# Shift and scale from transposed weights, and layer 0's input projection in skewed blocks

## The chip, the cores and the metric

The kernel runs on one core of one Trainium2 chip. The metric is the device time of one execution in microseconds (us). A core has a matrix engine (TensorE, PE in the profile; its weight loads are PEld), a vector engine (VectorE, DVE), an activation engine (ScalarE, ACT), GpSimd (POOL) and SyncE (SP), which here issues nearly all transfers from one queue, in order. Matrix products are accumulated in PSUM, eight banks of 128 x 512 float32; everything else lies in SBUF, 128 partitions wide.

## The reference

Two layers of an encoder on 256 positions of 2048 channels, all in float32. What the change touches is the modulation: six vectors of 2048 numbers per layer, made from one conditioning vector `c`, of which two pairs (shift and scale) act on a normalised input and two (gates) on a branch's output.

```python
c_act = silu(c)
for l in range(2):
    mod = (c_act @ w_mod[l] + b_mod[l]).reshape(bn, 6, 2048)
    shift_m, scale_m, gate_m, shift_f, scale_f, gate_f = ...
    h = layer_norm(x) * (1 + scale_m) + shift_m
    proj = h @ w_in[l]                    # 4288 columns: U, V, B, E, C, D below
    y = concat(gmlp(U, V), attention(B), short_conv(E, C), conformer_conv(D)) @ w_out[l]
    x = layer_norm(ALPHA * x + (1 + gate_m) * y, post_mix_g[l], post_mix_b[l])
    h = layer_norm(x) * (1 + scale_f) + shift_f
    y = (silu(conv3(h @ w_gate)) * (h @ w_val)) @ w_down[l]
    x = layer_norm(ALPHA * x + (1 + gate_f) * y, post_ffn_g[l], post_ffn_b[l])
```

`w_mod[l]` is 2048 x 12288 float32 (100.7 MB a layer), read once for a single row vector `c_act`.

## The kernel before

**Products.** Contraction runs over KT = 16 blocks of 128 channels (kt 0 to 15). Most weights are loaded into `wraw` tiles and split in two parts, `whi` by a cast on ACT (L437) and `wlo` by a subtraction on DVE (L438); activations are split likewise (`hT`, L457, L458), and each product is three products of the parts. Some weights (`wexact`, L421) are used unsplit in float32. All products are issued by `mm` (L94). Splits go through four `whi` and four `wlo` tiles, which the `wexact` tiles share.

**Raw tiles.** `raw_tile` (L81) hands out four SBUF tiles of 1 MiB in rotation. Weights to be split, modulation weights (`wmod`) and the gain rows of the norms (`gb`) all go through them, and SP issues a load when the tile it takes has been released.

**Modulation.** `mod_step` (L220) adds one block of a vector: weights 128 x width (partition = input channel) times the column `c_act[kt]`, added to a running tile `macc` or `qacc`, one DVE instruction. After 16 steps the partial sums of 128 partitions must be added and turned into columns: `mod_cols` (L170) does it with one matrix product per 128 channels (`ps_mod`), `mod_rows` (L194) with a split, products `ps_row` against ones, a copy `mrow` and four transposes (`ps_mod`, L205). Gates go through `gate_rows` (L265). `mod_stream` (L302) is a generator of steps; `stream` (L380) calls `pump` at each weight load, which takes steps at the phase's rate from `RATES` (L35). What is not ready when a norm wants it is fetched by `need` (L360).

**Layer 0's input projection** (`by_pieces`, L1224) must wait for layer 0's own shift and scale. It works in the five pieces of channels in `PIECES` (L45: 2, 2, 4, 4 and 4 blocks). For each, `mod_piece` (L228) loads 1 MiB units of `w_mod_first`, all 2048 input channels by the piece's columns; half of the first piece's steps are products on PE (`mod_row`, L247). When all units of a piece are in, `sums` turns them, `finish` (L1486) applies them to `hF` (the normalised, transposed input) and splits it, and the piece's products follow: group D (1024 columns) into four held PSUM banks, groups U, V, E (512 each) and, in the first four blocks, B (768) into banks that are copied out (`side`, L1252). D is unsplit for kt 0 to 3, U, V, E for kt 0 to 11. Groups B and C (L1344, L1351) follow with the mixers' own work, and then `out_proj`.

**Hand-over.** `out_proj` (L645) ends a layer half with a norm on DVE; `first_group` (L595) turns the result (`to_hT`, L566, transposes `ps_xT`, L576) and starts the next products. L571 to L573 make the first activation of each turn wait for the modulation. In layer 0's FFN the last four blocks (kt from LATE_KT = 12) of shift and scale come later, and `late` (L1390) does these blocks' products afterwards.

The instructions are put in order on each engine by the framework's scheduler, mostly near the order of the program; an engine runs its own in order.

Of the kernel before, what the change touches and what calls it, by code (L numbers as in the profile page):

```python
# [13 lines left out]
P = 128  # L14
D = 2048
# [20 lines left out]
    dict(B=1.634, C=1.9, out=1.7, first=1.2, up=0.68, down=0.83),  # L36
# [7 lines left out]

PIECES = ((0, 2), (2, 2), (4, 4), (8, 4), (12, 4))  # L45
# [9 lines left out]
LEAD = (2, 3, 1, 2, 2)  # L55
# [10 lines left out]
def encoder_kernel(ctx: ExitStack, tc: tile.TileContext, A: dict, consts: bass.AP, out: bass.AP):  # L66
# [83 lines left out]

    PM = []
# [16 lines left out]
    MOD, MOD_BY = {}, {}  # L168

    def mod_cols(l, m, k0, acc, row=None):  # L170

        n = acc.shape[1] // P
        ps = ms_tile("ps_mod")
        mm(ps[:, 0:n], ident, bcol[l][:, m * KT + k0 : m * KT + k0 + n], True, False)
        for j in range(n):
            mm(ps[:, j : j + 1], acc[:, j * P : (j + 1) * P], ones[:, 0:1], False, row is None)
            if row is not None:
                mm(ps[:, j : j + 1], row[:, j * P : (j + 1) * P], ones[0:1, 0:1], False, True)
        cols = keep.tile([P, n], F32, name=f"mod_{l}_{m}_{k0}")
        if m in (SHIFT_M, SHIFT_F):  # L180
            done = act.copy(cols, ps[:, 0:n])
        else:
            done = ident_act(cols, ps[:, 0:n], 1.0, ones[:, 0:1])
        for j in range(n):
            MOD[(l, m, k0 + j)] = cols[:, j : j + 1]
            MOD_BY[(l, m, k0 + j)] = done.ins.name
# [6 lines left out]

    def mod_rows(l, m, acc, n=4):  # L194

        ps = ms_tile("ps_row")
        parts = [x for c0 in range(0, n * 512, 1024) for x in halves(acc, c0, min(1024, n * 512 - c0))]
        for j, pair in enumerate(parts):
            for i, part in enumerate(pair):
                mm(ps[0:4, :], onesR[:, P + 4 * j : P + 4 * j + 4], part, j + i == 0, j + i == n)  # L200
        row = tmp_tile("mrow")
        act.copy(row[0:4, :], ps[0:4, :])
        ps = ms_tile("ps_mod")
        for i in range(4):
            pe.transpose(ps[:, 4 * i : 4 * i + 4], row[0:4, i * P : (i + 1) * P], ident[0:4, 0:4])  # L205
        cols = keep.tile([P, KT], F32, name=f"mod_{l}_{m}")
        done = dve.scalar_tensor_tensor(
            out=cols.rearrange("p (i j) -> p i j", i=4)[:, :, :n],
            in0=ps[:, 0:KT].rearrange("p (i j) -> p i j", i=4)[:, :, :n],
            scalar=0.0 if m in (SHIFT_M, SHIFT_F) else 1.0,  # L210
            in1=bcol[l][:, m * KT : m * KT + 4 * n].rearrange("p (j i) -> p i j", i=4),
            op0=ALU.add,
            op1=ALU.add,
        )
        for k in range(4 * n):
            at = 4 * (k % 4) + k // 4
            MOD[(l, m, k)] = cols[:, at : at + 1]
            MOD_BY[(l, m, k)] = done.ins.name
# [8 lines left out]

    def mod_piece(l, ms, k0, nkt, shared=False):  # L228


        n, width = len(ms), nkt * P
        nk = 2048 // (n * width)
        acc = tmpp.tile([P, D], F32, tag="macc", name="qacc", bufs=2)[:, : n * width]
        units = []
        box = {}

        def unit(u):
            raw = raw_tile("wmod").rearrange("p (k m c) -> p k m c", k=nk, m=n)
            nc.sync.dma_start(
                out=raw.rearrange("p k m c -> p (k m c)"), in_=A["w_mod_first"][16 * k0 * n * P // 2048 + u]  # L240
            )
            for k in range(nk):
                kt, w = u * nk + k, raw[:, k, :, :].rearrange("p m c -> p (m c)")
                if shared and k >= nk // 2:
                    if u == 0 and k == nk // 2:
                        box["row"] = acc_tile("mod_row")
                    mm(box["row"][0:1, :], cact[:, kt : kt + 1], w, u == 0 and k == nk // 2, kt == KT - 1)  # L247
                else:
                    mod_step(acc, w, kt, kt == 0)

        for u in range(KT // nk):
            units.append(lambda u=u: unit(u))

        def sums():
            row = None
            if shared:
                row = tmp_tile("mod_row")
                act.copy(row[0:1, :], box["row"][0:1, :])
            for i, m in enumerate(ms):
                at = slice(i * width, (i + 1) * width)  # L260
                mod_cols(l, m, k0, acc[:, at], None if row is None else row[0:1, at])

        return units, sums
# [15 lines left out]
    WITH_NORM = {(0, SHIFT_F), (0, SCALE_F), (1, SHIFT_M), (1, SCALE_M)}  # L279

    def settle(i=0):
        l, m, acc, k0, k1 = late.pop(i)
        if m in (GATE_M, GATE_F):
            gate_rows(l, m, acc)
        elif k0 == 0:
            mod_rows(l, m, acc, k1 // 4)
        else:
            mod_cols(l, m, k0, acc[:, k0 * P : k1 * P])

    def late_part(u, v, k0, nk, dst):  # L290
        nc.sync.dma_start(
            out=dst, in_=A["w_mod_late"][v - SHIFT_F, u, :, k0 : k0 + nk, :].rearrange("p k c -> p (k c)")
        )
        return [dst[:, k * 512 : (k + 1) * 512] for k in range(nk)]
# [3 lines left out]
    def load_late_first():  # L298
        for v in (SHIFT_F, SCALE_F):
            late_first[v] = late_part(0, v, 0, 2, slot("wlate")) + late_part(0, v, 2, 2, slot("wlate"))  # L300

    def mod_stream(order):  # L302

        held_back = {}
        for l, m in order:
            if (l, m) == (0, GATE_F):

                for u in range(4):  # L310
                    for v, acc in held_back.items():
                        ws = late_first[v] if u == 0 else late_part(u, v, 0, 4, raw_tile("wmod"))
                        for k in range(4):
                            mod_step(acc[:, LATE_KT * P :], ws[k], 4 * u + k, u + k == 0)
                        if u == 3:
                            late.append((0, v, acc, LATE_KT, KT))
                        yield
            while len(late) >= 2:
                if late[0][:2] in WITH_NORM:
                    yield  # L320
                else:
                    settle()
            acc = tmpp.tile([P, D], F32, tag="macc", name="macc", bufs=2)
            k1 = KT
            if l == 0 and m in (SHIFT_F, SCALE_F):
                held_back[m], k1 = acc, LATE_KT
            w = k1 * P
            for kt in range(KT):
                raw = raw_tile("wmod")
                nc.sync.dma_start(out=raw[:, :w], in_=A["w_mod"][l, kt * P : (kt + 1) * P, m * D : m * D + w])  # L330
                if kt == KT - 1 and m in (GATE_M, GATE_F):
                    row = raw_tile("brow")
                    nc.sync.dma_start(out=row[0:1, :], in_=A["b_mod"][l : l + 1, m * D : (m + 1) * D])
                mod_step(acc[:, :w], raw[:, :w], kt, kt == 0)
                if kt == KT - 1:
                    if m in (GATE_M, GATE_F):
                        dve.tensor_tensor(out=acc[0:1, :], in0=acc[0:1, :], in1=row[0:1, :], op=ALU.add)
                    late.append((l, m, acc, 0, k1))
                    if (l, m) in WITH_NORM:
                        settle(len(late) - 1)  # L340
                yield
                if kt == 1 and late and late[0][:2] not in WITH_NORM:
                    settle()

    mods = mod_stream(
        [(0, GATE_M), (0, SHIFT_F), (0, SCALE_F), (0, GATE_F), (1, SHIFT_F), (1, SCALE_F)]
        + [(1, SHIFT_M), (1, SCALE_M), (1, GATE_M), (1, GATE_F)]
    )
    pace = {"rate": 0.0, "credit": 0.0}

    def phase(l, name):
        pace["rate"] = RATES[l][name]
# [7 lines left out]
    def need(l, m, k1=KT):  # L360
        while (l, m, k1 - 1) not in MOD and (l, m) not in GATE:
            at = [i for i, x in enumerate(late) if x[:2] == (l, m) and x[4] == k1]
            if at:
                settle(at[0])
            else:
                assert next(mods, "end") != "end"
# [1293 lines left out]
```

## Time and profile before

| | us |
|---|---|
| median of 3 runs (2273.24 to 2274.61) | 2274.22 |
| time of the profiled execution | 2276.85 |
| its span, first to last instruction | 2275.1 |
| first product of group D | 28.14 |
| end of layer 0's input projection in pieces, first product of B after it | 190.07 |
| last product of group C, first of layer 0's output projection | 315.39 |

The mean granted TensorE clock of the execution was 0.992. Times below are counted from the span's start. In the profile's rows, "L94 PE MATMUL d<-whi,a 128\*128 128x512" is an instruction on PE issued by line 94, that writes `d` from `whi` and `a`; a part in brackets at the end is idle time ahead of it and what ended it. A float32 product shows as two instructions, a product of split parts as one. 201 MB of the 605 MB moved are modulation weights, by the issues that the page lists (32 and 128 of 1024 KB, 32 of 768 KB, 6 of 1024 KB and 4 of 512 KB).

### The profile page before, as it was taken

The numbers are of one execution on the slowest core, as the hardware profiler recorded it, in microseconds if no ns is written. First come the engines' busy times: TensorE is split into PE (matmuls) and PEld (weight loads), VectorE is DVE, ScalarE is ACT, GpSimd is POOL, SyncE is SP. The second block draws the span as 40 slices with busy tenths as digits, with TensorE's granted clock in tenths as the row PEclk, the third lists the DMA queues.
The fourth block names the chain that finished last, engine by engine and source line by source line (L and its number), as shares of the span: only waits on it lengthen the run. The fifth ranks groups of instructions, "written<-read, shape, count | busy, mean of one in ns | idle before, by whom it ended". The sixth has DMA issues, their size and how long they took to land.

```text
span 2275.1 us, 31298 instructions
## 1 busy us (share of the span) xinstructions
PE 2228.2 (98%) x12316; PEld 1918.6 (84%) x12316; DVE 1770.7 (78%) x2172; ACT 1108.9 (49%) x1655; POOL 25.8 (1%) x49
## 2 busy tenths in 40 slices
PE   7999999999999999999999999999999999999997
PEld 5789886798888888887789899889888888888886
DVE  6678988888888888989977899887675565565676
ACT  3346742354455444544554434545544454454553
POOL 0000000000000000000000000000000000000000
PEclk9999999999999999999999999999999999999999
DMA  9889789678888888898867566774675555555553
GB/s 394 346 358 349 279 318 360 250 288 314 305 308 313 314 321 326 307 335 329 290 237 258 197 232 254 280 262 175 233 258 185 188 188 199 185 188 201 185 186 148
DMA packets 94524, 605.19 MB, mean 266 GB/s; under 512 B 10692, under 2 KB 10884, under 8 KB 31524
## 3 DMA queue, kind: packets, MB, share of 16 engines
q1 hardware_dynamic: 94040, 602.29, 71.9%
q8 instruction: 96, 1.57, 0.3%
q0 software_dynamic: 336, 0.89, 0.1%
q14 instruction: 52, 0.43, 0.1%
HBM read 601.05 MB, written 2.10 MB: 265 GB/s over the span
## 4 chain that ended last, share of the span: by engine, by line
PE 89%; DVE 6%; issue 2%; ACT 2%; DMA 1%; POOL 0%; SPq 0%; DVEq 0%; ACTq 0%; POOLq 0%
PE g_c L94 22%; PE v_c L94 22%; PE d L94 19%; PE o L94 8%; PE D_c L94 4%; PE C_c L94 3%; PE U_c L94 1%; DVE wlo L438 1%; PE U L94 1%; PE V L94 1%; PE B_c L94 1%; DMA wmod<-in_w_mod_dram 1%; PE E_c L94 1%; PE E L94 1%; DVE macc L225 1%
## 5 line engine op out<-in xcount | busy, mean ns | idle before, releaser
L437 ACT CAST whi<-wraw 128x1024 fp32r<-128x1024 f32 (+1 forms) x632 | 643.8, 1043 | 751.5 <-PE g_c L94 221.0
L438 DVE TENSOR_TENSOR wlo<-wraw,whi 128x1024 fp32r<-128x1024 f32 (+1 forms) x632 | 750.5, 1214 | 291.1 <-ACT whi L437 269.7
L94 PE MATMUL d<-whi,a 128*128 128x512 f32 x1344 | 388.3, 390 | 2.3 <-ACT whi L437 2.3
L225 DVE SCALAR_TENSOR_TENSOR macc<-wmod,cact,macc 128x2048 f32<-128x2048 f32 (+2 forms) x174 | 353.7, 2033 | 31.3 <-DMA wmod<-in_w_mod_dram 27.5
L94 PE MATMUL v_c<-hT,whi 128*128 128x512 f32 (+1 forms) x1456 | 342.3, 382 | 0.0
L94 PE MATMUL g_c<-hT,whi 128*128 128x512 f32 (+1 forms) x1344 | 313.3, 380 | 0.0
L94 PEld LDWEIGHTS v_c<-hT,whi 128*128 128x128 f32 x1456 | 264.7, 189 | 48.5
L94 PEld LDWEIGHTS d<-whi,a 128*128 128x128 f32 x1344 | 251.8, 188 | 55.8 <-ACT whi L437 3.7
L94 PEld LDWEIGHTS g_c<-hT,whi 128*128 128x128 f32 x1344 | 243.5, 189 | 43.2
L94 PE MATMUL d<-wlo,a 128*128 128x512 f32 x672 | 233.4, 390 | 1.7 <-DVE wlo L438 1.7
L94 PE MATMUL v_c<-hT,wlo 128*128 128x256 f32 x1400 | 190.7, 283 | 0.0
L94 PEld LDWEIGHTS v_c<-hT,wlo 128*128 128x128 f32 x1400 | 183.2, 191 | 6.6
L94 PE MATMUL g_c<-hT,wlo 128*128 128x256 f32 x1280 | 175.8, 283 | 0.0
L94 PEld LDWEIGHTS g_c<-hT,wlo 128*128 128x128 f32 x1280 | 168.2, 191 | 5.9
L94 PEld LDWEIGHTS d<-wlo,a 128*128 128x128 f32 x672 | 126.2, 188 | 30.4 <-DVE wlo L438 4.3
L457 ACT CAST a<-g 128x512 fp32r<-128x512 f32 x132 | 80.6, 618 | 80.8 <-PE d L94 78.9
L94 PE MATMUL o<-whi,a 128*128 128x512 f32 x384 | 110.1, 391 | 0.0
L458 DVE TENSOR_TENSOR a<-g,a 128x512 fp32r<-128x512 f32 x132 | 87.6, 684 | 5.3 <-ACT a L457 5.3
L94 PE MATMUL D_c<-hT,whi 128*128 128x256 f32 x432 | 81.1, 292 | 6.3 <-ACT whi L437 4.3
L225 DVE SCALAR_TENSOR_TENSOR qacc<-wmod,cact,qacc 128x1024 f32<-128x1024 f32 (+1 forms) x67 | 74.3, 1109 | 15.0 <-DMA wmod<-in_w_mod_first_dram 13.0
L94 PEld LDWEIGHTS o<-whi,a 128*128 128x128 f32 x384 | 72.1, 188 | 15.7 <-issue 0.7
L94 PEld LDWEIGHTS D_c<-hT,whi 128*128 128x128 f32 x432 | 69.1, 199 | 8.1 <-ACT whi L437 5.4
(358 smaller groups left out, 2606.2 us busy)
## 6 DMA issues: line engine op xcount, KB each, us to landing
wraw<-in_ffn_w_up_dram SPq DMA_DIRECT2D x168, 1024.0 KB, 4.9
wmod<-in_w_mod_dram SPq DMA_DIRECT2D x128, 1024.0 KB, 6.2
wraw<-in_ffn_w_down_dram SPq DMA_DIRECT2D x88, 1024.0 KB, 4.8
wraw<-in_w_in_dram SPq DMA_DIRECT2D x33, 1024.0 KB, 6.9
wmod<-in_w_mod_first_dram SPq DMA_DIRECT2D x32, 1024.0 KB, 9.2
wraw<-in_w_out_dram SPq DMA_DIRECT2D x26, 1024.0 KB, 5.5
wmod<-in_w_mod_dram SPq DMA_DIRECT2D x32, 768.0 KB, 7.2
wexact<-in_w_in_dram SPq DMA_DIRECT2D x46, 512.0 KB, 7.7
```

Of the source, the lines that this page charges most:

```text
L94: pe.matmul(o, lhsT, rhs, start=start, stop=stop, skip_group_check=True)
L225: i = dve.scalar_tensor_tensor(out=acc, in0=w, scalar=col, in1=acc, op0=ALU.mult, op1=ALU.add)
L437: act.copy(hi[:, :m], r)
L438: i = dve.tensor_tensor(out=lo[:, :m], in0=r, in1=hi[:, :m].bitcast(F32), op=ALU.subtract)
L457: act.copy(hi, src)
L458: dve.tensor_tensor(out=lo, in0=src, in1=hi.bitcast(F32), op=ALU.subtract)
```

## The change

The weights of shift and scale are laid out transposed: 128 output channels on the partitions, 2048 input channels along the free dimension. One DVE instruction on such a tile multiplies it by `cB` (silu(c) repeated in all partitions, made once at the start) and its accumulator output gives the 128 finished sums as a column. The products, splits and transposes of `mod_cols` and `mod_rows` are gone; `mod_rows`, `mod_cols`, `mod_piece` and `mod_stream`'s special cases are removed. The bias is added to two columns at once, with the 1 of the scale added to the bias beforehand. Gates keep `mod_step`. Layer 0's input projection goes block by block: as soon as the two tiles (2 MiB) of block kt are summed, the block of `hF` is modulated and its D products can run; U, V, E and B keep the same groups of blocks, and follow later in a fixed list of turns, with weights fed 2 turns and modulation 4 turns ahead. Layer 1's shift and scale for the mixers now come before those for the FFN. The number of `macc` tiles falls from 2 to 1, and the waits of L571 to L573 are removed. In layer 0's FFN the last four blocks are done as eight tiles of 128 x 2048 in place of 32 steps of 128 x 512.

```diff
-    dict(B=1.634, C=1.9, out=1.7, first=1.2, up=0.68, down=0.83),
+    dict(B=1.3, C=1.5, out=1.3, first=1.2, up=0.68, down=0.83),
-PIECES = ((0, 2), (2, 2), (4, 4), (8, 4), (12, 4))
-LEAD = (2, 3, 1, 2, 2)
+LEAD, UNIT_LEAD = 2, 4
+    scales_up(0)
+    cB = keep.tile([P, D], F32, name="cB")
+    for q in range(4):
+        diag = tmp_tile("diag").rearrange("p (k j) -> p k j", k=4)
+        dve.tensor_tensor(
...
+        ps = acc_tile("ps_c")
+        mm(ps, ones, diag.rearrange("p k j -> p (k j)"), True, True)
+        act.copy(cB[:, q * 512 : (q + 1) * 512], ps)
+    def row_sum(raw, n, k0, total):
+        i = dve.scalar_tensor_tensor(
+            out=raw, in0=raw, scalar=1.0, in1=cB[:, k0 : k0 + n], op0=ALU.mult, op1=ALU.mult, accum_out=total
+        )
+        held(i, "mod")
+    def mod_unit(l, m, kt, total):
+        raw = raw_tile("wmod")
...
+        nc.sync.dma_start(out=raw, in_=A["w_mod_turned"][l, 2 * pair + m % 3, kt])
+        row_sum(raw, D, 0, total)
+    def mod_done(l, m, k0, n, total):
+        cols = keep.tile([P, 2, n], F32, name=f"mod_{l}_{m}_{k0}")
+        i = dve.tensor_tensor(
+            out=cols,
+            in0=total,
+            in1=bcol[l][:, m * KT : (m + 2) * KT].rearrange("p (h k) -> p h k", h=2)[:, :, k0 : k0 + n],
+            op=ALU.add,
+        )
...
-        i = ident_act(xn, X[t][:, k0 * P : k0 * P + n], r[:, 0:1], r[:, 1:2])
-        for m in (m_shift, m_scale):
-            for name in {MOD_BY[(l, m, k0 + j)] for j in range(nkt)}:
-                tc.add_manual_dep(i.ins, name, data_dep, reason="PSUM is free for the modulation first")
+        ident_act(xn, X[t][:, k0 * P : k0 * P + n], r[:, 0:1], r[:, 1:2])
...
+        def load_part(g, kts):
+            k0, nkt = kts[0], len(kts)
+            exact = k0 < PLAIN_KT
+            c0, width = (C_AG, 1024) if g == "D" else cols[g]
+            nk = nkt if g == "D" or exact else min(2048 // width, nkt)
+            for k in range(k0, k0 + nkt, nk):
+                parts = weights(w_in, k, nk, c0, width, exact or (g != "D" and k0 < LATE_KT))
...
+        turns = [("D", (0,)), ("U", (0, 1)), ("V", (0, 1)), ("D", (1,)), ("U", ()), ("V", ()), ("B", (0, 1)), ("E", (0, 1))]
+        turns += [("D", (2,)), ("D", (3,))] + [("U", (2, 3)), ("V", (2, 3))]
+        turns += [("D", (4,)), ("B", (2, 3)), ("D", (5,)), ("E", (2, 3)), ("D", (6,)), ("D", (7,))]
+        for k0 in (4, 8):
+            kts = tuple(range(k0, k0 + 4))
+            for i, g in enumerate("UVE"):
+                turns += [(g, kts), ("D", (k0 + 4 + i,))]
+            turns.append(("D", (k0 + 7,)))
+        turns += [(g, tuple(range(LATE_KT, KT))) for g in "UVE"]
...
+        for n, (g, kts) in enumerate(turns):
+            feed_to(n + 1 + (LEAD if n + LEAD < len(turns) - 2 else 0))
+            ahead = [k[0] for h, k in turns[: n + 1 + UNIT_LEAD] if h == "D"]
+            units_to(2 * ahead[-1] + 2)
...
+            if kts[:1] == (LATE_KT,) and g != "D":
+                next(mods)
...
+        def unit(kt, h):
...
+            mod_unit(0, SHIFT_M + h, kt, totals[kt][:, h, :])
+            if h == 0:
+                return
+            mod_done(0, SHIFT_M, kt, 1, totals[kt])
+            while len(rest) > 6 - 2 * (kt // 4):
+                rest.pop(0)()
+            x = hF[kt // 4][:, kt % 4, :]
+            sc, sh = MOD[(0, SCALE_M, kt)], MOD[(0, SHIFT_M, kt)]
+            i = dve.tensor_scalar(out=x, in0=x, scalar1=sc, scalar2=sh, op0=ALU.mult, op1=ALU.add)
+            if kt >= PLAIN_KT and kt % 2 == 1:
+                split(hT[kt // 2], hF[kt // 4][:, kt % 4 - 1 : kt % 4 + 1, :])
```

More of the change, by code (lines that the diff above doesn't have):

```diff
@@ L166, in load_params @@
                 tc.add_manual_dep(i.ins, behind.ins.name, data_dep, reason="the pieces' weights go first")
[L168 to L186, printed above, removed]
+        if l > 0:
+            scales_up(l)
+    MOD = {}
+    def row_sum(raw, n, k0, total):
[5 more added lines that the diff above has]
+        raw = raw_tile("wmod")
+        pair = PAIRS.index((m, m + 1)) if m in (SHIFT_M, SHIFT_F) else PAIRS.index((m - 1, m))
+        nc.sync.dma_start(out=raw, in_=A["w_mod_turned"][l, 2 * pair + m % 3, kt])
[7 more added lines that the diff above has]
+            op=ALU.add,
+        )
+        for h in range(2):
+            for k in range(n):
+                MOD[(l, m + h, k0 + k)] = cols[:, h, k : k + 1]
+        return i
     def halves(acc, c0, width=1024):
@@ L192, in halves @@
         return [(hi[:, i : i + 512], lo[:, i : i + 512]) for i in range(0, width, 512)]
[L194 to L218, printed above, removed]
     def mod_step(acc, w, kt, first):
@@ L226, in mod_step @@
         held(i, "mod")
[L228 to L263, printed above, removed]
     def gate_rows(l, m, acc):
@@ L278, in encoder_kernel, with settle @@
     late = []
[L279 to L294, printed above, removed]
+    def settle():
+        gate_rows(*late.pop(0))
@@ L296, in encoder_kernel @@
     late_first = {}
     def load_late_first():
[L299 to L319, printed above, removed]
-                    yield
-                else:
-                    settle()
[L323 to L348, printed above, removed]
+        for m in (SHIFT_F, SCALE_F):
+            for h in range(2):
+                half = slot("wlate")
+                nc.sync.dma_start(out=half, in_=A["w_mod_turned"][0, 2 + m % 3, LATE_KT, :, h * 1024 : (h + 1) * 1024])
+                late_first[(m, h)] = half
+    def columns(l, m, k0, k1):
+        for ka in range(k0, k1, 4):
+            total = smallp.tile([P, 2, 4], F32, tag="total", name="total")
+            for kt in range(ka, ka + 4):
+                for h in range(2):
+                    if (l, m, kt) == (0, SHIFT_F, LATE_KT):
+                        two = smallp.tile([P, 2], F32, tag="two", name="two")
+                        for i in range(2):
+                            row_sum(late_first[(m + h, i)], 1024, i * 1024, two[:, i : i + 1])
+                        dve.tensor_tensor(out=total[:, h, 0:1], in0=two[:, 0:1], in1=two[:, 1:2], op=ALU.add)
+                    else:
+                        mod_unit(l, m + h, kt, total[:, h, kt - ka : kt - ka + 1])
+                    if (kt, h) == (ka + 3, 1):
+                        mod_done(l, m, ka, 4, total)
+                    yield
@@ new lines, in gate_steps @@
+    def gate_steps(l, m):
+        while late:
+            settle()
+        acc = tmpp.tile([P, D], F32, tag="macc", name="macc", bufs=1)
+        for kt in range(KT):
+            raw = raw_tile("wmod")
+            nc.sync.dma_start(out=raw, in_=A["w_mod_gates"][l, m // 3, kt])
+            if kt == KT - 1:
+                row = raw_tile("brow")
+                nc.sync.dma_start(out=row[0:1, :], in_=A["b_mod"][l : l + 1, m * D : (m + 1) * D])
+            mod_step(acc, raw, kt, kt == 0)
+            if kt == KT - 1:
+                dve.tensor_tensor(out=acc[0:1, :], in0=acc[0:1, :], in1=row[0:1, :], op=ALU.add)
+                late.append((l, m, acc))
+            yield
@@ new lines, in mod_stream @@
+    def mod_stream():
+        parts = [
+            gate_steps(0, GATE_M),
+            columns(0, SHIFT_F, 0, LATE_KT),
+            columns(0, SHIFT_F, LATE_KT, KT),
+            gate_steps(0, GATE_F),
+            columns(1, SHIFT_M, 0, KT),
+            columns(1, SHIFT_F, 0, KT),
+            gate_steps(1, GATE_M),
+            gate_steps(1, GATE_F),
+        ]
+        for part in parts:
+            for n, _ in enumerate(part):
+                yield
+                if n == 1 and late:
+                    settle()
@@ L361, in need @@
         while (l, m, k1 - 1) not in MOD and (l, m) not in GATE:
-            at = [i for i, x in enumerate(late) if x[:2] == (l, m) and x[4] == k1]
-            if at:
-                settle(at[0])
+            if late and late[0][:2] == (l, m):
+                settle()
             else:
@@ L1274, in by_pieces @@
         sums["B"] = [both[i // 2][:, (i % 2) * 512 : (i % 2 + 1) * 512] for i in range(3)]
-        made = {0: between(0)}
-        rest_of_x = made[0][2]
-        counts = [0] + [2 * n for _, n in PIECES[1:]]
-        begun = {"units": 0}
-        def steps_to(q, share, lead=0):
-            upto = sum(counts[:q]) + int(counts[q] * share + 0.999) + lead if q < len(PIECES) else 0
-            while begun["units"] < upto:
-                at, before = 1, begun["units"]
-                while at < len(PIECES) and before >= counts[at]:
-                    before -= counts[at]
-                    at += 1
-                if at == len(PIECES):
-                    next(mods)
-                else:
-                    if at not in made:
-                        made[at] = between(at)
-                    made[at][0][before]()
-                begun["units"] += 1
@@ L1452, in normed_T, with quarter @@
             scale.append(r)
-        def quarter(t, q, behind=None):
+        def quarter(t, q):
             r = scale[t]
@@ L1458, in quarter @@
             xn = tmp_tile("xn")
-            i = ident_act(xn, X[t][:, q * 512 : (q + 1) * 512], r[:, 0:1], r[:, 1:2])
-            if behind is not None:
-                tc.add_manual_dep(i.ins, behind.ins.name, order_dep, reason="the first piece goes first")
+            ident_act(xn, X[t][:, q * 512 : (q + 1) * 512], r[:, 0:1], r[:, 1:2])
             ps = ms_tile("ps_xT")
@@ L1498, in finish @@
                 load_params(0, i)
-            for kt in range(max(k0, PLAIN_KT), k0 + nkt, 2):
-                split(hT[kt // 2], hF[kt // 4][:, kt % 4 : kt % 4 + 2, :])
-        return units, finish, rest
+        return [lambda kt=kt, h=h: unit(kt, h) for kt in range(KT) for h in range(2)], rest
     def needs(l, *ms, k1=KT):
```

160 lines of the change are left out of this document (74 added, 86 removed).

## The prediction

> **What bounds the kernel now.** I read the page's busy line first, then busy time by stage, then what the first stage waits for, because the change is concentrated there.
>
> ```profile
> PE 2228.2 (98%) x12316; PEld 1918.6 (84%) x12316; DVE 1770.7 (78%) x2172; ACT 1108.9 (49%) x1655; POOL 25.8 (1%) x49
> ```
>
> PE is busy 98% of the span, but these ends are modelled, so I cut the span where its work changes (columns as in the first line):
>
> ```profile
> core 0: us, PE busy (x) PEld busy (x) DVE busy (x) ACT busy (x) POOL busy (x), PEclk, DMA share, GB/s
> 0.00:28.14 28.14, 14.75 (x53) 6.68 (x53) 13.50 (x26) 10.38 (x19) 3.79 (x17) 0.97 0.92 370
> 28.14:84.63 56.49, 53.69 (x244) 44.23 (x244) 33.76 (x35) 26.07 (x48) 0.00 (x0) 0.95 0.95 387
> 84.63:190.07 105.44, 101.08 (x605) 88.10 (x606) 73.62 (x63) 46.01 (x70) 1.65 (x3) 0.97 0.86 337
> 190.07:315.39 125.32, 123.54 (x602) 106.09 (x601) 116.44 (x138) 83.23 (x188) 4.27 (x7) 1.00 0.85 321
> 315.39:416.27 100.88, 100.17 (x358) 64.60 (x356) 83.02 (x105) 27.34 (x39) 2.15 (x3) 1.00 0.91 337
> ```
>
> From 190 us on PE has hardly a gap, so work removed from PE there counts in full, and other engines' savings hardly count. The first 190 us are different: no group product runs before 28.14, and transfers are heavy. The transfer view of those 190 us, in 40 slices:
>
> ```profile
> GB/s 118 428 433 412 416 423 417 413 421 418 415 413 411 416 428 419 382 18 33 412 359 431 414 421 428 160 258 344 417 428 417 416 419 418 195 391 345 229 186 353
> DMA packets 12360, 67.80 MB, mean 357 GB/s; under 512 B 1559, under 2 KB 1735, under 8 KB 6078
> ```
>
> Transfers run at about 420 GB/s, except in three holes (near 82, 120 and from 160 us). The waits of the same stretch say why:
>
> ```profile
> DVE hF L1494 <- ACT mod L97: 17.9, 3, 9.9
> SPq L239 <- DVE qacc L225: 44.2, 22, 4.2
> ```
>
> DVE stood 17.9 us at piece ends, waiting for columns that come only when PE has finished the old piece and run `ps_mod`. Meanwhile no raw tile is released and SP issues nothing. So the first stage is bound by turns at piece ends, not by one engine.
>
> **The change part by part.** *Start.* Today four units must land, then PE and ACT turn them:
>
> ```profile
> 6.82 2.47 DVE L1445 BATCH_NORM_STATS2 st_in<-x 128x6 f32<-128x512 f32 x4 [6.82 <-DMA x<-in_x_dram]
> 14.74 1.54 DVE L225 SCALAR_TENSOR_TENSOR qacc<-wmod,cact,qacc 128x512 f32<-128x512 f32 x2 [0.80 <-DMA wmod<-in_w_mod_first_dram]
> 19.74 1.54 DVE L225 SCALAR_TENSOR_TENSOR qacc<-wmod,cact,qacc 128x512 f32<-128x512 f32 x2 [0.96 <-DMA wmod<-in_w_mod_first_dram]
> 28.14 3.78 PE L94 MATMUL D_c<-hF,wexact 128*128 128x256 f32 x8 [0.98 <-ACT hF L97]
> ```
>
> DVE waited for the second unit until 14.74 and for the fourth until 19.74, 2.5 us a unit. Afterwards two are enough. A row sum's price stands in these rows (ns, minimum/median/maximum):
>
> ```profile
> L719 DVE SCALAR_TENSOR_TENSOR x<-x,rs_o0p,gb x4: 748/749/751, 409.8 to 413.2; 128x512 f32<-128x512 f32 x4
> L719 DVE DVE_READ_ACCUMULATOR x<-x,rs_o0p,gb x4: 84/84/85, 410.5 to 413.9; 128x1 f32 x4
> L716 DVE SCALAR_TENSOR_TENSOR x<-x,mv_o0p,gb x4: 743/748/749, 408.5 to 411.8; 128x512 f32<-128x512 f32 x4
> L225 DVE SCALAR_TENSOR_TENSOR macc<-wmod,cact,macc x174: 743/2344/2354, 153.1 to 1678.8; 128x2048 f32<-128x2048 f32 x120, 128x1536 f32<-128x1536 f32 x30, 128x512 f32<-128x512 f32 x24
> L223 DVE TENSOR_SCALAR macc<-wmod,cact 128x2048 f32<-128x2048 f32 x8 | 10.3, 1282 | 5.2 <-DMA wmod<-in_w_mod_dram 4.6 <-PE ps_mod L94 0.5
> ```
>
> With an accumulator output an instruction takes 749 ns against 748 without, and reading it 84 ns. I take 2.4 us for 2048 elements. First D product: statistics end at 12.6, two sums 4.8, bias and modulation about 0.6 make 18.0; the four `diag` products for `cB` (0.7 each, as L716 at 512 elements) fit ahead of 6.82 only if the bias `bcol`, which DVE reads first, is there by then; else they add 3. I take 19.5, between 18 and 21.
>
> On this very instruction the Trainium skill speaks against the change: its "Vector Engine (DVE) Microarchitecture Reference", section "Points that are easy to get wrong", says that the scalar-tensor-tensor form with two SBUF sources wider than bf16 halves throughput, with no read port left for accumulator readback. By the trace two float32 sources already cost 2344 ns where one costs 1282, and the accumulator costs no second halving. If the rule meant another halving, a sum would cost 4.7 us; rival 4 has that time.
>
> *Products of the first stage.* These don't change, apart from `mod_row` and `ps_mod`. From the chain of waits (start, us, what), then PE's timeline:
>
> ```profile
> 36.53 1.73 PE D_c L94 x8
> 64.65 3.45 PE U L94 x16
> 71.53 5.18 PE B L94 x24
> 120.01 1.69 PE ps_mod L94 x16
> ```
> ```profile
> 178.55 0.40 PE L94 MATMUL D_c<-hT,whi 128*128 128x256 f32 x2
> 181.43 0.40 PE L94 MATMUL E<-hT,whi 128*128 128x256 f32 x2
> 187.19 0.40 PE L94 MATMUL D_c<-hT,whi 128*128 128x256 f32 x2
> 190.07 9.23 PE L94 MATMUL B_c<-hF,wexact 128*128 128x256 f32 x42
> ```
>
> Unsplit, a block of D costs 2 x 1.73 = 3.46 and one of U, V or E 3.45/2 = 1.73 (V is as wide); two of B cost 5.18. Split, a block of D takes 190.07 - 187.19 = 2.88 and the last four of E 5.76. In all 4 x 3.46 + 36 x 1.73 + 2 x 5.18 + 12 x 2.88 + 3 x 5.76 = 138 us. Between 28.14 and 190.07 lie 162 us, so 24 go to other things: `ps_mod` (1.69 for 16; some 90 are 9.5), transposes, waits, a lower clock. The `ps_mod` and the waits at piece ends go; transposes stay, and the start after an idle stretch stays slow (8 D products took 3.78 at 28.14, not 1.73). I leave 10 of 24, bounds 3 and 24. The stage then ends at 19.5 + 138 + 10 = 167.5 in place of 190.1: **-22.6 us** (-8 to -31).
>
> *Transfers and DVE there.* The same 67.8 MB have to come; at 420 GB/s that is 161 us from 2 us on, so end 163. Transfers and PE limit alike, which is why I don't go below 10. DVE: 35 sums of 2.4 = 84, splits, modulation and statistics about 40, makes 124 of 167: not the bound. SP's queue: each D block loads 0.5 MiB into a 1 MiB raw tile, so a block takes three of four raw tiles. Behind a sum that waits for its tile stand the `wlo` splits, on which D waits; two blocks of lead cover that, and without lead it is rival 3.
>
> *B, C and layer 0's output projection.* The rates fall (1.634, 1.9, 1.7 to 1.3, 1.5, 1.3) because 24 full steps replace 32 of 1536 wide: 40 x 2.4 = 96 against 16 x 2.34 + 32 x 1.81 = 95 us on DVE, the same bytes. PE, with 1.8 us of gaps in 125 and 0.7 in 101, hides them; I take 0, and if that cover is gone, as where the first stage's end moves and these stages begin earlier, the price is DVE's: 116.4 us of work in 125.3 leaves 9 us of room. Two `mod_rows` leave PE there, four more until 1120. Their price from PE's timeline:
>
> ```profile
> 1113.95 0.40 PE L94 MATMUL ps_row<-mlo,onesR 128*4 128x512 f32 x1 [0.27 <-DVE mlo L458]
> 1114.19 0.39 PE L94 MATMUL ps_row<-mhi,onesR 128*4 128x512 f32 x1
> 1114.42 0.40 PE L94 MATMUL ps_row<-mlo,onesR 128*4 128x512 f32 x1
> 1117.36 0.41 PE L205 MATMUL ps_mod<-cst,mrow 4*128 4x4 f32 x4
> ```
>
> 0.23 us from start to start; eight (six in layer 0), 0.4 for transposes and 0.3 of waiting: 2.5 each, four **-10** (-8 to -11), and 1.75 each, two **-3.5** (-2 to -4).
>
> *Hand-over at 416.* 6 x 1.3 + 8 x 1.5 + 12 x 1.3 = 35.4 steps plus three in the first stage are 38 of 40; two sums (4.8 us) now run in `need`, ahead of the norm's reads on DVE, in raw tiles next to the two `gb`.
>
> ```profile
> 405.97 0.69 DVE L683 TENSOR_TENSOR yg<-o,gate 128x512 f32<-128x512 f32 x1 [5.25 <-PE o L94]
> ```
>
> DVE idles 5.25 us there, which hides them if they have landed; uncovered they cost 4.8, and FFN weights queue behind `gb`. I take **+1** (0 to +5).
>
> *The late four blocks.* From PE's timeline:
>
> ```profile
> 477.18 1.03 PE L94 MATMUL ps_mod<-onesR,macc 128*128 128x1 f32 x8
> 480.53 1.97 PE L576 MATMUL ps_xT<-cst,xn 128*128 128x128 f32 x8 [1.20 <-ACT xn L97]
> 483.12 9.18 PE L94 MATMUL g_c<-hF,wexact 128*128 128x256 f32 x32 [0.62 <-ACT hF L97]
> ```
>
> From 477.2 to 492.3 PE does 32 products that at U's rate are 6.9, after `ps_mod`, ACT's columns and transposes that had to wait for them. Without these waits the transposes go earlier and about 2 us of modulation remain: 9 for 15, **-6** (-9 to -2).
>
> *Second layer half.* Where DVE is tight before 1130, PE waited:
>
> ```profile
> PE d L94 <- ACT whi L437: 2.3, 3, 1.7
> PE d L94 <- DVE wlo L438: 1.7, 3, 0.6
> ```
>
> The splits of `mod_rows` (1.2 us each on DVE) leave this stretch: **-2** (-4 to 0). In layer 1's own time no shift or scale step is left to change: 0. That layer 1's mixer vectors now come ahead of the FFN's costs nothing, since both were ready before 1130 as it is (the last `ps_row` stand at 1116). One `macc` tile in place of two makes a gate wait for the gate before it to be split; layer 0's two gates have 32 steps between them and layer 1's are taken at 0.3 to 0.6 a weight load, so 0. POOL's loads of constants and parameters wait for the last block now as before, and nothing reads them before the end of the stage.
>
> **Sum:** -22.6 - 3.5 + 1 - 6 - 10 - 2 = -43.1 us on a span of 2275.1, so 2232; the profiled execution took 2276.85, 1.75 above its span and 2.6 above the median shown, so **2231 us** as the runs count.
>
> **The rivals.** (1) *Forecast*, 0.64: 2212 to 2250.
>
> (2) *Transfers keep their holes*, 0.20. With half-filled raw tiles, SP may stand as often as now: 67.8 MB at the 357 GB/s of today end at 190, and the first stage gains nothing, give or take 10. With the other terms (-20.5) the total is -10 to -31: 2243 to 2264, middle 2254. For it: SP already waited 44.2 us for DVE to release tiles. Against it: it did so in slices of 413 to 428 GB/s, and the holes belong to the piece ends.
>
> (3) *Blocks run one after another*, slower, 0.10. If a block's loads are issued only when the last block's tiles are released, each costs landing plus sum plus modulation. The page has
>
> ```profile
> wmod<-in_w_mod_first_dram SPq DMA_DIRECT2D x32, 1024.0 KB, 9.2
> ```
>
> 9.2 from issue to landing, 2.4 and 1.0: 12.6 a block against 8.6 of products (138/16). Sixteen such from 17 on and 17 us for the last U, V, E end at 236, +46; with the other terms (-20.5) 2300. It decides from (190.1 + 20.5 - 34)/16 = 11 us a block: above that the kernel is slower, 2274 to 2300.
>
> (4) *The accumulator halves DVE*, 0.02: 128 sums at 4.7 (twice 2344 ns) in place of 2.4 are 294 us more on an engine busy 1770.7. First stage: 35 x 4.7 + 40 = 205 us of DVE, end near 218; 190 to 416: 199 us of DVE plus 92 make 291 for 226; later sums fill the 18% that DVE had free. Above 2350.
>
> 0.04 is left for better than 2212.
>
> **How the numbers follow.** Forecast and the upper part of (2) lie in 2212 to 2262, some 0.8. About 0.2% (4.5 us) is what a measurement of this kernel can tell from no change. Faster: 0.64 + 0.20 + 0.04, less a little of (2), 0.86; same: the edges of (2) and (3), 0.06; slower: the rest of (3), and (4), 0.08.
>
> **What would show it.** Right: the first D product near 19 us, the first B product after the pieces near 167, no transfer slice under 300 GB/s from 20 to 140 us, `ps_row` and `mod_row` gone, sums near 2.35 us, about 9 us in place of 15 at the late blocks. Wrong: sums of 4 us or more (4); SP's waits for raw tiles next to holes in the transfers (2); PE idle at each block until a sum lands (3).

## The result and the profile after

The changed kernel takes 2260.85 us (median of 4 runs, 2257.45 to 2261.62) against 2274.14 (4 runs, 2273.24 to 2274.61): a ratio of 0.9939, 95% interval 0.9922 to 0.9956, 13.3 us faster. The forecast was 2231, so some 30 us of the 43 are missing. The profiled execution of after took 2257.45 (span 2255.7), the fastest of its four, and that of before 2276.85, above the other runs shown, so the two traces differ by 19.4 us and the medians by 13.3.

The page's busy line of the changed kernel, and its busy time by stage, cut at the same events as before's:

```profile
PE 2198.7 (97%) x12128; PEld 1899.5 (84%) x12128; DVE 1762.5 (78%) x2260; ACT 1088.1 (48%) x1617; POOL 28.0 (1%) x49
```
```profile
core 0: us, PE busy (x) PEld busy (x) DVE busy (x) ACT busy (x) POOL busy (x), PEclk, DMA share, GB/s
0.00:20.07 20.07, 7.32 (x17) 3.31 (x17) 13.47 (x26) 9.92 (x16) 5.60 (x17) 0.90 0.88 347
20.07:182.15 162.08, 149.46 (x789) 124.33 (x790) 112.30 (x128) 73.08 (x117) 3.36 (x6) 0.96 0.93 364
182.15:307.19 125.04, 123.52 (x599) 105.98 (x598) 112.70 (x134) 75.04 (x174) 2.86 (x5) 1.00 0.83 320
307.19:408.20 101.01, 95.74 (x338) 62.93 (x336) 84.77 (x114) 24.07 (x34) 2.16 (x3) 0.99 0.91 347
408.20:477.81 69.61, 68.66 (x544) 67.27 (x545) 59.33 (x83) 32.16 (x48) 1.54 (x2) 0.97 0.78 298
477.81:914.60 436.79, 436.79 (x2539) 387.28 (x2538) 381.23 (x459) 224.26 (x336) 0.00 (x0) 1.00 0.83 314
914.60:1166.02 251.42, 244.55 (x1064) 199.03 (x1063) 221.28 (x259) 123.09 (x157) 1.47 (x2) 0.99 0.81 300
```

The first D product stands at 20.07 instead of 28.14. But from there to the first product of B after the pieces (182.15) it takes 162.1 us, as long as before (190.07 - 28.14 = 161.9). PE had nothing to do for 12.6 of them, against 7.2 before (56.49 - 53.69 and 105.44 - 101.08 in the prediction's rows): its busy time fell by 5.3 us, from 154.8 to 149.5, and its idle time grew by as much. From both PE timelines, first instruction to first instruction:

| stretch | before, us | after, us | difference | forecast |
|---|---|---|---|---|
| start to the first D product | 28.1 | 20.1 | -8.1 | -8.6 |
| first D product to the end of the pieces | 161.9 | 162.1 | +0.2 | -13.9 |
| B, C | 125.3 | 124.7 | -0.6 | 0 |
| layer 0's output projection, to its last product | 100.8 | 96.1 | -4.7 | -3.5 |
| from there to the first product of FFN group g | 2.0 | 7.0 | +5.1 | +1 |
| to the v products after the late four blocks | 73.7 | 67.9 | -5.9 | -6 |
| to the first product of the second FFN product | 441.5 | 436.6 | -4.8 | -5 |
| second FFN product | 252.8 | 251.6 | -1.2 | -7 |
| layer 1, to the first product of its FFN | 335.0 | 337.3 | +2.3 | 0 |
| the rest | 754.0 | 752.4 | -1.5 | 0 |

Two terms failed by 5 us or more, and one hand-over by 4. The transfers of the first 190 us, in 40 slices:

```profile
GB/s 112 421 422 420 413 417 417 414 414 414 426 392 44 402 414 347 245 391 304 372 375 417 426 392 403 350 250 407 431 416 410 410 349 256 397 365 108 395 409 415
DMA packets 13804, 69.26 MB, mean 365 GB/s; under 512 B 1716, under 2 KB 1892, under 8 KB 8290
```

There are holes again, at other places: near 59, 78, 126, 158 and 173 us. The waits up to 185 us (in total, times, longest), then SP's own:

```profile
DVE wlo L397 <- ACT whi L396: 25.8, 12, 7.6
ACT sumE L1228 <- PE E L94: 18.3, 8, 5.1
ACT sumU L1228 <- PE U L94: 17.6, 6, 6.5
ACT sumV L1228 <- PE V L94: 15.6, 5, 5.5
PE D_c L94 <- ACT hT L416: 11.1, 6, 4.0
```
```profile
SPq L200 <- DVE wmod L192: 25.4, 9, 7.2
SPq L200 <- DVE wlo L397: 25.4, 8, 9.2
SPq L385 <- DVE wlo L397: 17.5, 4, 5.5
```

Before's wait of `hF` for ACT's `mod` (17.9 us) is gone. In its place DVE waits 25.8 us for ACT to cast weights (`whi`; 9.7 before), and SP waits for DVE to release raw tiles. Why ACT is late shows in its timeline, with DVE's and PE's next instructions behind it:

```profile
76.02 0.59 ACT L1223 COPY E<-sumE 128x512 f32<-128x512 f32 x1
80.00 0.59 ACT L1228 COPY sumE<-E 128x512 f32<-128x512 f32 x1 [3.39 <-PE E L94]
80.61 0.59 ACT L1223 COPY U<-sumU 128x512 f32<-128x512 f32 x1
81.72 0.59 ACT L1228 COPY sumE<-E 128x512 f32<-128x512 f32 x1 [0.52 <-PE E L94]
82.34 0.59 ACT L1223 COPY U<-sumU 128x512 f32<-128x512 f32 x1
82.87 1.04 ACT L396 CAST whi<-wraw 128x1024 fp32r<-128x1024 f32 x1
83.81 0.61 ACT L416 CAST hT<-hF 128x512 fp32r<-128x512 f32 x1
```
```profile
83.94 1.23 DVE L397 TENSOR_TENSOR wlo<-wraw,whi 128x1024 fp32r<-128x1024 f32 x1 [5.74 <-ACT whi L396]
```
```profile
84.48 1.92 PE L94 MATMUL D_c<-hT,whi 128*128 128x256 f32 x5 [2.79 <-ACT hT L416]
```

A copy of a side group's sum (`sumE<-E`, L1228) waits for PE to finish the group. Behind it in ACT's order stand the cast of the next D weights and the cast of `hT`. Here they run only when PE has nothing left; DVE's subtraction waits for them, the row sums stand behind the subtraction, and raw tiles stay taken. The ring closes: PE waits for a cast that stands behind a copy that waited for PE.

### The profile page after: what moved, and what is told of

Read it like the earlier page. It is cut to its first block, busy times and chain, and to the rows that moved or that the text cites. A ratio compares the mean times of both kernels' runs of the same rounds, so it can differ in the third digit from the quotient of the medians.

```text
span 2255.7 us, 30853 instructions
## 1 busy us (share of the span) xinstructions
PE 2198.7 (97%) x12128; PEld 1899.5 (84%) x12128; DVE 1762.5 (78%) x2260; ACT 1088.1 (48%) x1617; POOL 28.0 (1%) x49
## 4 chain that ended last, share of the span: by engine, by line
PE 80%; DVE 5%; issue 1%; ACT 1%; DMA 0%; POOL 0%; DVEq 0%; POOLq 0%; ACTq 0%
PE g_c L94 22%; PE v_c L94 22%; PE d L94 19%; PE o L94 7%; PE C_c L94 3%; PE D_c L94 2%; PE U_c L94 1%; DVE wlo L397 1%; PE B_c L94 1%; PE E_c L94 1%; DVE convD L826 1%; DVE wmod L192 0%; PE ps_xT L532 0%; DVE a L417 0%; DMA wraw<-in_w_out_dram 0%
## 5 line engine op out<-in xcount | busy, mean ns | idle before, releaser
L192 DVE SCALAR_TENSOR_TENSOR wmod<-wmod,cB 128x2048 f32<-128x2048 f32 x126 | 286.9, 2285 | 17.5 <-DMA wmod<-in_w_mod_turned_dram 17.4
L227 DVE SCALAR_TENSOR_TENSOR macc<-wmod,cact,macc 128x2048 f32<-128x2048 f32 x60 | 140.7, 2344 | 8.0 <-DMA wmod<-in_w_mod_gates_dram 7.9
```

What stands on the lines that cost most here:

```text
L192: i = dve.scalar_tensor_tensor(out=raw, in0=raw, scalar=1.0, in1=cB[:, k0 : k0 + n], op0=ALU.mult, op1=ALU.mult, accum_out=total)
L227: i = dve.scalar_tensor_tensor(out=acc, in0=w, scalar=col, in1=acc, op0=ALU.mult, op1=ALU.add)
```

## The experiments

The number compared is the time from the first D product to the first product of B after the pieces: 162.1 us in the changed kernel. Its spread can be read from two later kernels with the same instructions in this stage: 162.5 (b_out145) and 167.3 (b_updown, where the granted clock was 0.97 from 100 to 150 us, 1.00 in the other). Differences of under 5 us in one profile are therefore not resolved. A kernel for which no median is given ran once. Theory Q says that the order of the queues is the cause; rivals are that the raw tiles are too few (R, the mechanism that the prediction's second rival named) and that DVE has too much to do (V).

**Casts on another engine.** In the first stage only, `whi` and `hT` are cast on POOL (or on DVE, with `dve.tensor_copy`); ahead of B, `caster[0]` is `act.copy` again:

```diff
+    caster = [act.copy]
-            act.copy(hi[:, :m], r)
+            caster[0](hi[:, :m], r)
-        act.copy(hi, src)
+        caster[0](hi, src)
+        caster[0] = pool.tensor_copy
```

> Changed kernel, but in the first stage the casts of weights (whi) and of activations (hT) run on POOL instead of ACT. The changed kernel's first stage ends at 182 us (first product of B after the pieces), with DVE waiting 25.8 us for whi and holes in the transfers. Theory Q (queue order): the casts stand in ACT's order behind copies that wait for PE; DVE's subtraction waits for the cast, the next row sums wait behind the subtraction, so raw tiles come free late and SP stops. Then the casts on an engine of their own run as soon as weights land, DVE's waits for whi fall under 8 us, most transfer slices between 20 and 140 us stay over 390 GB/s, and the stage ends at 170 to 176. Theory R (raw tiles are too few, half of each D tile is empty) and theory V (DVE has too much to do at once): no change in the order matters, the end stays at 180 to 184. A POOL cast of 128x1024 that takes over 2.5 us would hide the effect.

> As a_cast_pool, with these casts on DVE, ahead of the subtraction. Q: the wait for ACT is gone, but DVE gets some 18 casts of 128x1024 and 6 of 128x512 more, about 1.2 and 0.7 us each as its subtractions, 20 us in all on 112 of 162; the stage ends at 172 to 179. R: 180 to 184. V: later than now, 186 to 200.

Measured: 149.9 us with POOL (170.18 - 20.32), 150.5 with DVE (170.99 - 20.49). Casts on DVE, the first B product, the transfers, what PE still waited for, and the cast's own row:

```profile
170.99 1.25 PE L94 MATMUL B_c<-hF,wexact 128*128 128x256 f32 x5
```
```profile
GB/s 97 423 422 418 412 417 419 412 419 408 422 404 422 417 383 307 354 436 398 424 414 416 350 392 420 413 425 414 411 339 369 410 415 345 220 357 422 406 415 408
```
```profile
PE D_c L94 <- DVE hT L418: 3.0, 3, 1.0
PE D_c L94 <- DVE hT L417: 1.1, 3, 0.7
```
```profile
L397 DVE CAST whi<-wraw x18: 682/686/694, 51.5 to 159.2; 128x1024 fp32r<-128x1024 f32 x18
```

One slice alone is left under 300 GB/s, at 220 near 164 us, and PE waits 4.1 us for `hT` instead of 11.8. Twelve microseconds came back although DVE had more to do (24 casts, 18 at 0.69 and 6 at 0.42, make 15 us). V falls. Nor is it the price of a cast: POOL's took 1.37 us (median) where ACT's take 1.05. The stage with casts on DVE ended at 171.0, a little before the 172 to 179 expected, since that range took 1.2 us for a cast. Timed, the kernel with casts on DVE is 15 us faster than the change:

> a_cast_dve again, timed: 2246 to 2250 as the runs count if the 12 us of the first stage are all that it changes.

Measured: 2245.48 us median (2245.32 to 2247.27, 4 runs), ratio to before 0.9868 (0.9851 to 0.9884), just under the 2246 to 2250 expected; the stage took 150.9.

**A fifth raw tile.**

```diff
-    rawp = ctx.enter_context(tc.tile_pool(name="rawp", bufs=4))
+    rawp = ctx.enter_context(tc.tile_pool(name="rawp", bufs=5))
...
-    tmpp = ctx.enter_context(tc.tile_pool(name="tmpp", bufs=4))
-    actp = ctx.enter_context(tc.tile_pool(name="actp", bufs=10))
+    tmpp = ctx.enter_context(tc.tile_pool(name="tmpp", bufs=3))
+    actp = ctx.enter_context(tc.tile_pool(name="actp", bufs=9))
```

> Changed kernel with five raw tiles of 1 MiB instead of four (room for it is taken from one activation tile and one 128x512 temporary, which the first stage does not need). R: SP no longer stands, the holes go, the stage ends at 168 to 174. Q: SP runs 2.5 us of transfer further ahead, but DVE stands as long for ACT's casts; the stage ends at 178 to 182. Later stages may lose some us for the two tiles taken, which is no part of the question.

Measured: 164.7 us (185.38 - 20.69), an end later than either range, and within the spread of the changed kernel. DVE stood as long as ever for ACT, and SP for DVE's subtractions (29.6 us at L200, 25.4 in the change):

```profile
DVE wlo L397 <- ACT whi L396: 30.8, 12, 9.6
```

R falls: a tile more did not let SP run on. What the two tiles taken away cost by themselves was not measured.

**Short sums.** In the first stage `n` is 64, elsewhere 2048:

```diff
-        row_sum(raw, D, 0, total)
+        row_sum(raw[:, :n], n, 0, total)
```

> Changed kernel whose row sums of the first stage read only 64 of the 2048 input channels (the rest of layer 0's first shift and scale is left out of the sum), while the same tiles are loaded and released in the same order: 0.1 us instead of 2.29 each, 30 sums between 20 us and the end of the stage, 66 us less DVE. V: the end falls to 168 to 172. Q: DVE's waits for whi remain (20 us or more) and with them holes in the transfers; the end falls only by what DVE needs to catch up after each wait, to 175 to 180. R: 178 to 182.

Measured: 162.4 us (180.45 - 18.05), nothing gained, so V falls once more. The end, 180.4, lies just above Q's range and within R's, which the fifth tile rules out. DVE was busy 68.4 us of the first 190, half of the 133.6 in the changed kernel, and yet

```profile
DVE wlo L397 <- ACT whi L396: 22.5, 13, 9.1
```

**The reverse: copies on DVE.**

```diff
-                    act.copy(o, total)
+                    dve.tensor_copy(o, total)
...
-                    act.copy(total, o)
+                    dve.tensor_copy(total, o)
```

> The reverse of a_cast_dve: in the first stage the copies of the side groups (U, V, E, B: total to bank and bank to total) run on DVE, and the casts stay on ACT. Theory Q (what matters is which instructions stand behind a copy that waits for PE): now the row sums themselves and the subtractions stand behind the copies in DVE's order, so raw tiles come free later still; DVE waits for PE 40 us or more, and the stage takes 165 to 185 us from the first D product to the first product of B after the pieces (the changed kernel 162, casts on DVE 150). If it had been ACT's load or the price of its casts instead, relieving ACT of some 45 copies would shorten the stage to 150 to 158.

Measured: 177.5 us (198.39 - 20.88), 15 us worse than the change, and 2275.11 us in all: the change's whole gain is gone. ACT is relieved (43.1 us busy in the stage instead of 73.1), and it gets slower, though DVE's waits for `whi` fall to 2.9 us now that no copy stands ahead of the casts. By Q that is because the copies that wait for PE now stand in front of the row sums. DVE also has 31 us more to do, so part of the 15 may be that load; but it is busy 81% of this stage (143.0 of 177.5), where with the casts it was 85% (128.1 of 150.5) in a faster one. From the waits of this kernel, DVE's then SP's:

```profile
DVE sumU L1228 <- PE U L94: 8.7, 4, 2.7
DVE sumB L1228 <- PE B L94: 7.0, 4, 4.5
```
```profile
SPq L200 <- DVE wmod L192: 51.0, 16, 6.3
```

DVE's waits for PE come to 21.6 us over the four groups, not to the 40 expected; SP's wait for the row sums doubled from 25.4 to 51.0.

**Only the order on ACT.**

```diff
-            act.copy(hi[:, :m], r)
+            last_cast[0] = act.copy(hi[:, :m], r)
...
+        def behind_cast(i):
+            if last_cast[0] is not None:
+                tc.add_manual_dep(i.ins, last_cast[0].ins.name, order_dep, reason="the casts go first")
...
-                    act.copy(o, total)
+                    behind_cast(act.copy(o, total))
...
-                    act.copy(total, o)
+                    behind_cast(act.copy(total, o))
```

> Changed kernel, with only an order added on ACT: a copy of a side group stands behind the last cast of weights that was emitted, where it stood ahead of it in most cases; the casts of activations (hT) stay where they were. All work stays on its engine. Q: DVE's waits for whi fall from 25.8 to under 12 us, the stage takes 152 to 159 us. If it is ACT as an engine and not the order: 161 to 166. If copies that now wait for a cast hold up PE's next bank: 160 or more with new waits of U, V, E on ACT.

Measured: 162.9 us (183.41 - 20.55), so this expectation of Q was missed, and DVE's waits for `whi` fell to 19.2, not under 12:

```profile
DVE wlo L398 <- ACT whi L397: 19.2, 11, 6.0
PE D_c L94 <- ACT hT L417: 8.6, 4, 2.9
```

The casts of `hT` still stood behind copies that wait for PE, ACT's waits for U, E and V came to as much as before (51.9 us against 51.5), and PE now waited 2.1 us for a copy into a U bank. The time lies in the ranges of both other readings, ACT as an engine and copies that hold up PE's banks, so this run doesn't tell them from an order that moved too few casts. This order didn't open the ring. Whether another order on ACT alone would has not been tried; what is shown is that casts on a queue without such copies do.

**Each half alone.** `whi` alone on DVE, or `hT` alone.

> a_cast_dve, but only the casts of weights (whi) go to DVE; those of activations (hT) stay on ACT. The changed kernel takes 162 us from the first D product to the first product of B after the pieces, a_cast_dve 150.5. If raw tiles held back by late weight casts were the main part: transfers keep 400 GB/s and more between 60 and 150 us, PE still waits for hT (11 us in the changed kernel) for 4 to 9 us, and the stage takes 152 to 156. If PE's waits for hT are the main part: 157 to 161.

> The other half: only hT casts go to DVE, whi stays on ACT. If late weight casts are the main part: DVE's waits for whi stay over 18 us, the holes in the transfers stay, and the stage takes 157 to 162. If PE's waits for hT are the main part: PE's waits before D fall from 11 us to 4 or less, and the stage takes 151 to 156.

Measured: `whi` alone 158.1 us (177.92 - 19.79), `hT` alone 166.8 (186.71 - 19.88). PE still waited 6.0 us for ACT's `hT` in the first, and DVE 35.5 us for ACT's `whi` in the second:

```profile
PE D_c L94 <- ACT hT L417: 6.0, 4, 1.8
```
```profile
DVE wlo L398 <- ACT whi L397: 35.5, 10, 8.1
```

The two don't fit either reading: 158.1 lies in the range for `hT` as the main part, with transfers that fell to 242 GB/s near 74 us instead of keeping 400, and 166.8 lies above all ranges. Against the spread of 162.1 to 167.3, a gain of `whi` alone is likely, and `hT` alone gained nothing. So the halves don't add up to the 12 us of both. That the ring stays partly closed as long as one link runs through ACT would explain it; it is argued, not shown.

**The hand-over and the second FFN product.** Only rates of layer 0 change:

```diff
-    dict(B=1.3, C=1.5, out=1.3, first=1.2, up=0.68, down=0.83),
+    dict(B=1.3, C=1.5, out=1.45, first=1.2, up=0.68, down=0.83),
...
+    dict(B=1.3, C=1.5, out=1.3, first=1.2, up=0.78, down=0.6),
```

The first line with a plus is b_out145, the second b_updown. In the changed kernel two row sums ran between the norm's steps on DVE, and PE waited:

```profile
397.20 2.29 DVE L192 SCALAR_TENSOR_TENSOR wmod<-wmod,cB 128x2048 f32<-128x2048 f32 x1
399.42 0.75 DVE L675 SCALAR_TENSOR_TENSOR x<-x,rs_o0p,gb 128x512 f32<-128x512 f32 x1
400.09 2.29 DVE L192 SCALAR_TENSOR_TENSOR wmod<-wmod,cB 128x2048 f32<-128x2048 f32 x1
```
```profile
408.20 1.97 PE L532 MATMUL ps_xT<-cst,xn 128*128 128x128 f32 x8 [5.27 <-ACT xn L97]
```

> Changed kernel with layer 0's out rate at 1.45 in place of 1.3, so that no row sum is left for the norm at the end of layer 0's output projection. Theory H (the two sums that ran between the norm's steps, 397.20 to 399.42 and 400.09 to 402.30 us, hold up the hand-over): PE's idle time before the first ps_xT there falls from 5.27 us to 0.7 to 1.5, and the time from the first product of out (306.84) to the first of FFN group g (409.96), now 103.1, falls to 98 to 99.5. Rival (the tiles are short: two of four hold gb, so two more sums in out take tiles that its weights need): the idle time goes, but out's products take as much longer, 102 to 104.

Measured: PE's idle time there is 0.77 us, and from the first out product to the first of g it takes 98.7:

```profile
405.97 1.36 PE L532 MATMUL ps_xT<-cst,xn 128*128 128x128 f32 x8 [0.77 <-ACT xn L97]
```

As a whole this kernel's span was 2255.3, only 0.4 less: B and C took 1.5 us longer and the late blocks 2.5. With the casts moved as well (below) the gain is kept.

Over the whole second FFN product, PE's busy time fell from 248.2 us in the kernel before to 244.6, but its idle time grew from 4.6 to 6.9. The row of the kernel before, then the second chunk in the changed kernel, where DVE was full:

```profile
933.40:1186.20 252.80, 248.24 (x1091) 199.98 (x1089) 226.91 (x237) 127.87 (x164) 1.47 (x2) 1.00 0.82 302
1046.00:1108.00 62.00, 56.42 (x239) 43.79 (x237) 61.21 (x77) 31.92 (x41) 0.00 (x0) 1.00 0.85 311
```
```profile
PE d L94 <- DVE wlo L397: 4.6, 7, 1.9
PE d L94 <- ACT whi L396: 2.0, 2, 1.7
```

> Changed kernel with layer 0's rates up=0.78, down=0.6 in place of 0.68, 0.83: some eight row sums (2.37 us each, 19 us of DVE) move from the second FFN product, where DVE is full (61.2 of 62 us in its second chunk), to the first, where it has 13% free. Theory D (the saved mod_rows were given back there because DVE sets the pace): the second product, now 251.4 us (914.60 to 1166.02), takes 245 to 248, and the first stays at 436.8 within 1.5. Rival (its pace is set by transfers or by the order of the casts): the second product stays at 250 to 252.

Measured: the second FFN product takes 243.1 us instead of 251.6, a larger gain than expected, the first 438.6 instead of 436.6, a little more than the 1.5 us allowed, and no wait of PE is left between 960 and 1120 us.

**All three.** Casts on DVE in the first stage, and the three rates:

> a_cast_dve with both rates (out 1.45, up 0.78, down 0.6). If the three causes are separate and add: 150 us from the first D product to the end of the first stage, hand-over idle near 1, second FFN product 245 to 248; against the changed kernel -12, -4 and -4 us, so 2238 to 2243 as the runs count. If DVE, now with 20 us of casts more, is short in the stages that follow, the gains overlap and it stays at 2243 to 2250.

Measured: 2236.64 us median (2236.01 to 2240.12, 4 runs), ratio to before 0.9833 (0.9817 to 0.9850): 38 us faster than before, 24 faster than the change, and a little below the 2238 to 2243 expected if the three gains add. First stage 150.4 us, from out's last product to g 2.0 (7.0 in the change), second FFN product 245.2. It is the best version found.

## Why the prediction was wrong, step by step

- **Start**: right, 20.07 for 19.5. The sum's price was right as well (2.4 predicted, and the accumulator doesn't halve DVE):

```profile
L192 DVE SCALAR_TENSOR_TENSOR wmod<-wmod,cB x126: 2272/2285/2294, 13.9 to 1088.1; 128x2048 f32<-128x2048 f32 x126
L192 DVE DVE_READ_ACCUMULATOR wmod<-wmod,cB x126: 74/82/90, 16.1 to 1090.3; 128x1 f32 x126
```

  The Trainium skill's "Vector Engine (DVE) Microarchitecture Reference", section "Points that are easy to get wrong", names a halving for this form with two SBUF sources that are not bf16. Here it is in the 2344 ns that two float32 sources cost before, where one cost 1282; 2285 with the accumulator shows no second one.
- **Products of the first stage**: this is the step that failed. "I leave 10 of 24, bounds 3 and 24": 24.1 remained (162.1 - 138), at the upper bound. The step took the waits at piece ends as gone with the pieces, and moved the sums past the queues of ACT and DVE without asking what stands in them: the prediction looked at SP's queue behind a sum, and at DVE's splits behind it, but not at the casts behind the copies on ACT. The PE work did go (5.3 us of busy time), but PE's idle time rose from 7.2 to 12.6 us. With the casts out of that queue 12.5 of the 24 remained (150.5 - 138), close to the 10 predicted, and 4.1 of idle time. So what the prediction removed from PE was right, and a new wait took the place of the one removed.
- **Transfers and DVE there**: "DVE ... not the bound" was right (short sums gained nothing), but 420 GB/s in mean was too much: the stage moved 364 GB/s, and 393 with casts on DVE. The sign named, no slice under 300 GB/s from 20 to 140 us, failed: 44 and 245 and 250 appear. The time of rival 2 (2243 to 2264) came true, and so did its sign, SP's waits for raw tiles next to holes; the reason it gave, half-filled raw tiles, did not hold, since a fifth tile didn't help.
- **B and C, output projection**: B and C right (-0.6 for 0); the output projection a little past its bound of -4 (-4.7 for -3.5, that is 2.4 us for each of two `mod_rows` and not 1.75).
- **Hand-over**: mis-sized. "DVE idles 5.25 us there, which hides them if they have landed" failed on its condition. The loads of the two weight tiles were issued from 380.95 on, after two of the four raw tiles had gone to `gb`, and took 12.0 us to land (median), when DVE's idle time of 8.7 us was ending (392.66). The sums ran inside the norm: +5.1 for +1, just past the bound.
- **Late four blocks**: right (-5.9 for -6).
- **Four `mod_rows`, DVE-tight stretch**: the two in the first FFN product came out (-4.8 for -5). The two in the second, and the 2 us of DVE, did not (-1.2 for -7), since 61.2 us of DVE in 62 set the pace there; less PE work mostly made PE wait, 6.9 us instead of 4.6. The kernel b_updown, which moves DVE's work away, bears this out. The prediction saw that DVE was tight there, and yet counted PE's savings in full.
- **Layer 1**: +2.3 for 0. PE waited 4.0 us for `xn` at its hand-over, 2.0 before; the cause is open.

Rival 3 (blocks one after another) did not occur, as the sign for it didn't: PE's gaps stand at `hT` casts, not at sums that wait for landing.

## What to carry to other kernels

When a stage is cut finer, list for every engine what will stand behind each instruction that waits for another engine: a copy that waits for PE should not share a queue with work on which PE's next products, or the release of load tiles, depend. Work taken from PE counts only where PE is the last to be ready; in a window where DVE is full, it counts little (1.2 of 7 us here) until DVE's work is moved. Steps left over "for the norm" are free only if their data has landed before the norm begins, so a rate should be set so that none is left.

## What the runs showed of the hardware that was not expected

An idle stretch of PE can cost more than its own length. The changed kernel ahead of the gap of 4.0 us that ends at 65.91, and behind it; behind the gap of 2.8 us that ends at 84.48; and behind one of 1.2 us that ends at 121.73:

```profile
50.00:60.00 10.00, 10.00 (x44) 7.26 (x43) 2.22 (x5) 5.37 (x9) 0.00 (x0) 1.00 0.72 290
65.91:70.80 4.89, 4.74 (x20) 4.45 (x21) 4.63 (x5) 0.90 (x1) 0.00 (x0) 0.50 1.02 417
70.80:80.00 9.20, 9.20 (x57) 8.51 (x56) 7.26 (x10) 3.54 (x7) 0.00 (x0) 1.00 0.85 307
84.48:87.86 3.38, 3.26 (x13) 2.97 (x14) 3.38 (x4) 0.89 (x1) 0.00 (x0) 0.50 0.89 338
121.70:126.00 4.30, 4.27 (x33) 4.08 (x34) 4.03 (x3) 2.46 (x3) 0.00 (x0) 1.00 0.55 172
```

PE was busy again after 65.91, but at a granted clock of 0.50 for 4.9 us, after 1.00 ahead of the gap: some 2 us more. After 84.48 it was 0.50 for 3.4 us; behind the gap of 1.2 us it stayed at 1.00. The Trainium skill's "TensorE: Matmul & The Clock Gate", section "What's actually happening", has the clock at half until PE has been busy for about 3.4 us. The trace agrees behind the second gap, and shows a longer time behind the first. The length of a gap alone doesn't decide: behind gaps of 2.3 us the kernel before shows 0.52 (108.20 to 111.70) and the kernel with copies on DVE 1.00 (110.11 to 113.50). Of the 11.2 us that the stage is shorter with the casts on DVE (150.9, PE busy 146.5), 8.3 are idle time and 2.9 are busy time.

A cast of 128x1024 from float32 took 1.05 us on ACT, 0.69 on DVE and 1.37 on POOL (medians; on POOL up to 3.09), where DVE's subtraction of the same size, with two sources, takes 1.2. The expectation took 1.2 for DVE's cast too.
